# Two-part accumulation for the B, C and inner-channel streams, and a reworked decay, in a hybrid SSD trunk

## Chip, cores and metric

The kernel runs on one core of one Trainium2 chip. The metric is device time in microseconds of one execution; lower is better. Runs shown before are given as median, lowest and highest of three.

## What is computed

A trunk of two layers over 256 tokens and 2048 channels in float32. Layer 0 mixes tokens with a Mamba-2 state-space mixer (SSD), layer 1 with a short gated convolution; each is followed by a gated convolutional feed-forward block, and an RMSNorm closes. The change lies in the SSD mixer:

```python
def ssd_mixer(u, w_in, conv_w, conv_b, dt_bias, a_log, d_skip, norm_w, w_out):
    z, xbc, dt_raw = split(u @ w_in)                 # 4096 | 4096 + 1024 + 1024 | 64 columns
    xbc = silu(causal_dwconv(xbc, conv_w, conv_b))   # width 4
    xs, bm, cm = split(xbc)                          # inner channels, B, C (8 groups x 128 states)
    dt = softplus(dt_raw + dt_bias); a = -exp(a_log)
    y = ssd_chunked(xs, dt, a, bm, cm)               # two chunks of 128 tokens, 64 heads
    ...
# in ssd_chunked
    cs = cumsum(dt * a)                              # per head and chunk, falls
    decay[l, s] = exp(cs[l] - cs[s]) for s <= l, else 0
    y_diag = (C B^T * decay) @ (x * dt)
```

## The kernel before

**Precision by parts.** Every weight tile and every activation is split into a high part (a cast to the matmul's float32r format) and a low remainder. A product is then high x high + high x low + low x high: weight high against activation high and low, weight low against activation high. An activation tile `hl` holds its high part in columns 0 to 255 (the 256 tokens) and its low part in columns 256 to 511.

**Weights.** `plan` lists all 880 weight units in the order in which they are used; a unit is 256 rows by 512 columns (two blocks `k` of 128 rows, four blocks `t` of 128 columns). SyncE (SP) issues one 512 KB DMA per unit into `raw` (4 buffers). ScalarE casts it to `wh` (L302), VectorE subtracts for `wl` (L303); `wh` and `wl` have 4 buffers each.

**Streams.** `stream()` (L323) does one product of 512 output columns over all 2048 input rows: 8 units, 64 steps `(t, k)`. Its sums lie in two PSUM tiles ("main", three buffers of two banks in all), one for each pair of column blocks. With `one=True` a step is three matmuls of 256 columns into the same 256 columns of the tile: weight high x activation high (L354), weight high x activation low (L355), weight low x activation high (L340). With `one=False` it is one matmul of 512 columns, high and low side by side (L357), and the one of 256 (L340); the tile then holds two parts that must be added. When the last unit is through, `evac` is called for each of the two tiles: `scaled(pt, r, True)` multiplies the 256 columns by the row norm in one VectorE instruction (L412), while `scaled(pt, r)` first copies the upper part out with ScalarE (L404), adds on VectorE (L406), and then multiplies (L415). Then follow the width-4 convolution (L426 on ScalarE, L428 on VectorE) and SiLU.

Four kinds of stream run in the mixer: B and C (`bc_stream`, four streams, each for four groups), the inner channels (`xs_stream`, one for each of 8 groups), the gate (`z_stream`, 8, `one=False`), and the output projection (`residual_stream`, `one=False`). The first B stream is special: it is interleaved by hand with the preparation of `x` (`before=x_pair`) and its order is pinned. The later parts of the trunk use `late_stream`, whose steps are always 512 + 256 columns.

**Decays.** `ssd_decay` (L661) makes the masked decay for two heads: a DMA on SP's queue spreads the cumulative sums of two heads over all partitions (`cbc`, 256 KB, two buffers); six VectorE instructions of 128 columns subtract or add the token's own sum and clip at zero (L668, L670, L672); one ScalarE instruction exponentiates 768 columns (L674); one VectorE instruction multiplies by C B^T (L676). It is called 32 times. The tiles `m` that it fills have three buffers and are read by the matmuls L707 and L715.

**Order.** The Tile framework makes the order on each engine from its own simulated timeline; the first stream's instructions are pinned, and the late streams' matmuls are chained by `follow`. Elsewhere the framework may interleave the matmuls of one stream with those of the next and with the small products of the SSD core.

Of the kernel before, what the change touches and what calls it, by code (L numbers as in the profile page):

```python
# [8 lines left out]
F32 = mybir.dt.float32  # L9
F32R = mybir.dt.float32r  # L10
I32 = mybir.dt.int32
AF = mybir.ActivationFunctionType
ALU = mybir.AluOpType
# [3 lines left out]
P = 128  # L17
T = 256
D = 2048
NKD = D // P  # L20
DI = 4096
NG = 8
GC = DI // NG
NH = 64
HPG = NH // NG
DS = 128
CONVD = DI + 2 * NG * DS
W_SSD = 4
# [11 lines left out]
def trunk_kernel(ctx, tc, a, out):  # L40
    nc = tc.nc
    mm = nc.tensor.matmul
    act = nc.scalar.activation
    tt = nc.vector.tensor_tensor
    stt = nc.vector.scalar_tensor_tensor
    ts = nc.vector.tensor_scalar
# [29 lines left out]
    def uid(s):  # L76
        n_id[0] += 1
        return f"{s}_{n_id[0]}"

    def pair_tmp(tag="tp", pool=None):  # L80
        return (pool or tmp).tile([P, 2, T], F32, tag=tag, name=uid(tag))
# [7 lines left out]
    xspool = mixer.enter_context(tc.tile_pool(name="xspool", bufs=3))  # L89
# [128 lines left out]
    def rep2(t):  # L218
        return t.unsqueeze(1).to_broadcast([P, 2, T])
# [72 lines left out]
    def load_unit():  # L292
        i = len(units)
        if i == len(raws):
            load_raw()
        raw, raws[i] = raws[i], None
        wh = wpool.tile([P, KU, COLS], F32R, tag="wh", name=uid("wh"))
        wl = wpool.tile([P, KU, COLS], F32R, tag="wl", name=uid("wl"))
        units.append((wh, wl))

        def half(ks, put):
            put(nc.scalar.copy(wh[:, ks, :], raw[:, ks, :]))  # L302
            put(tt(  # L303
                out=wl[:, ks, :], in0=raw[:, ks, :], in1=wh[:, ks, :].bitcast(F32),
                op=ALU.subtract,
            ))

        if i == 0:
            return half
        with tc.high_priority(0 if i < NKD // KU else None):  # L310
            half(slice(0, KU), pin if i < NKD // KU + 2 else lambda ins: ins)

    def weight_unit(c0, kc, ahead=WB - 1):

        i = taken[0]
        assert plan[i][1:] == (c0, kc), (plan[i], c0, kc)
        taken[0] += 1
        while len(units) < min(i + ahead + 1, len(plan)):
            load_unit()
        got, units[i] = units[i], None  # L320
        return got

    def stream(c0, hls, kcs, evac, one=False, before=None):  # L323

        pts = [psm.tile([P, 2, 512], F32, tag="main", name=uid("main")) for _ in range(2)]
        n = len(kcs)
        put = (lambda ins: ins) if before is None else pin  # L330
        for u in range(0, n, KU):
            order = [(t, k) for t in range(4) for k in range(KU)]
            if before is not None and u == 0:
                before(0)
                order.sort(key=lambda tk: tk[1])
            wh, wl = weight_unit(c0, kcs[u], WB - 1 if before is None else 0)

            def low(t, k):
                i = u + k
                put(mm(  # L340
                    pts[t // 2][:, t % 2, 0:T], wl[:, k, t * P : (t + 1) * P],
                    hls[i // 2][:, i % 2, 0:T], start=False, stop=(i == n - 1),
                ))

            for at, (t, k) in enumerate(order):
                if before is not None and at == (0 if u else 2) and u + KU < n:
                    before(u // KU + 1)
                i = u + k
                o = pts[t // 2][:, t % 2, :]
                hl = hls[i // 2][:, i % 2, :]  # L350
                lw = slice(t * P, (t + 1) * P)
                first = i == 0
                if one:
                    put(mm(o[:, 0:T], wh[:, k, lw], hl[:, 0:T], start=first, stop=False))  # L354
                    put(mm(o[:, 0:T], wh[:, k, lw], hl[:, T : 2 * T], start=False, stop=False))  # L355
                else:
                    put(mm(o, wh[:, k, lw], hl, start=first, stop=False))  # L357
                if before is not None:
                    low(t, k)
                elif k == KU - 1:  # L360
                    for q in range(KU):
                        low(t, q)
        if before is not None:
            before(n // KU)
        if taken[0] < len(plan):
            while len(units) < min(taken[0] + WB - 1, len(plan)):
                load_unit()
        for p in range(2):
            evac(p, pts[p])
# [39 lines left out]
    def scaled(pt, r, one=False, tag="tp", pool=None):  # L409
        if one:  # L410
            s = pair_tmp(tag, pool)
            tt(out=s, in0=pt[:, :, 0:T], in1=rep2(r), op=ALU.mult)  # L412
            return s
        s = pair_sum(pt)
        tt(out=s, in0=s, in1=rep2(r), op=ALU.mult)  # L415
        return s

    def conv(s, width, wname, nk, k0, bname=None, tag="tp", pool=None):

        y = pair_tmp(tag, pool)  # L420
        for j in range(2):
            w = pcol(wname, (width - 1) * nk + k0 + j)
            if bname is None:
                act(y[:, j, :], s[:, j, :], AF.Copy, scale=w)
            else:
                act(y[:, j, :], s[:, j, :], AF.Identity, bias=pcol(bname, k0 + j), scale=w)  # L426
            for d in range(1, width):
                stt(  # L428
                    out=y[:, j, d:T], in0=s[:, j, 0 : T - d],
                    scalar=pcol(wname, (width - 1 - d) * nk + k0 + j),  # L430
                    in1=y[:, j, d:T], op0=ALU.mult, op1=ALU.add,
                )
        return y
# [27 lines left out]
    xp, xhl = [], []  # L461
    ss = small.tile([P, 2, 4], F32, tag="ss", name="ss")
    first = {}
# [48 lines left out]
    NCX = CONVD // P  # L512

    def bc_stream(g, o, before=None):

        res = []

        def evac(p, pt):
            k0 = DI // P + o * NG + g + 2 * p
            s = scaled(pt, first["r0"], True)  # L520
            y = conv(s, W_SSD, "ssdw", NCX, k0, "ssdb", "bc", bcpool)
            act(y, y, AF.Silu)
            res.append(y)

        stream(2 * DI + o * NG * DS + g * DS, xhl, range(NKD), evac, True, before)
        return res

    load_raw()
# [9 lines left out]
    for _ in range(2):  # L538
# [3 lines left out]
        out=dtw, in_=s_in[:, DI + CONVD :].rearrange("(k p) h -> p k h", p=P)  # L542
    ))

    def row_bcast(src, n, tag):
# [8 lines left out]
    r_tok, r0 = first["r_tok"], first["r0"]  # L554
# [4 lines left out]
        out=dtw, in0=dtw,  # L559
        in1=prm[i0][:, o0 : o0 + NKD].unsqueeze(2).to_broadcast([P, NKD, NH]), op=ALU.mult,  # L560
# [20 lines left out]
    for c in range(2):  # L581
        stt(
            out=v[:, c * NH : (c + 1) * NH], in0=ps[:, c * NH : (c + 1) * NH],
# [22 lines left out]
    cs = cpool.tile([P, 2, NH], F32, tag="cs", name="cs")  # L606
# [3 lines left out]
    rem = cpool.tile([P, NH], F32, tag="rem", name="rem")  # L610
# [14 lines left out]
    sp = mixer.enter_context(tc.tile_pool(name="sp", bufs=2))  # L625
    decpool = mixer.enter_context(tc.tile_pool(name="decpool", bufs=3))

    def xs_stream(g):
        res = [None, None]

        def evac(p, pt):
            y = conv(scaled(pt, r0, True), W_SSD, "ssdw", NCX, g * 4 + 2 * p, "ssdb", "xs", xspool)
            act(y, y, AF.Silu)
            res[p] = y

        stream(DI + g * GC, xhl, range(NKD), evac, True)
        return res

    def z_stream(g):
# [19 lines left out]
        return cb  # L659

    def ssd_decay(g, part, cb):  # L661
        h0 = g * HPG + part * 2
        cbc = sp.tile([P, 2, 2, P], F32, tag="cbc", name=uid("cbc"))
        nc.sync.dma_start(out=cbc, in_=cs_d[:, h0 : h0 + 2, :].partition_broadcast(P))
        m = decpool.tile([P, 2, 3, P], F32, tag="decay", name=uid("decay"))
        for h in range(2):
            hi = h0 + h
            ts(out=m[:, h, 0, :], in0=cbc[:, 0, h, :], scalar1=cs[:, 0, hi : hi + 1], scalar2=0.0,  # L668
               op0=ALU.subtract, op1=ALU.min)
            ts(out=m[:, h, 1, :], in0=cbc[:, 1, h, :], scalar1=rem[:, hi : hi + 1], scalar2=0.0,  # L670
               op0=ALU.add, op1=ALU.min)
            ts(out=m[:, h, 2, :], in0=cbc[:, 1, h, :], scalar1=cs[:, 1, hi : hi + 1], scalar2=0.0,  # L672
               op0=ALU.subtract, op1=ALU.min)
        act(m, m, AF.Exp)  # L674
        mf = m.rearrange("p h j l -> p h (j l)")
        tt(  # L676
            out=mf, in0=mf,
            in1=cb.rearrange("p j l -> p (j l)").unsqueeze(1).to_broadcast([P, 2, 3 * P]),
            op=ALU.mult,
        )  # L680
        return m
# [87 lines left out]
    for g in range(NG):  # L769
# [5 lines left out]
        m = [ssd_decay(g, part, cb) for part in range(4)]  # L775
        xs = xs_stream(g)
# [44 lines left out]
    xhl, nhl = nhl, []  # L821
# [11 lines left out]
    xhl, nhl = nhl, []  # L833
# [32 lines left out]
    xhl = nhl  # L866
# [30 lines left out]
    for part in range(2):  # L897
        lo, hi = FPARTS[part]
        hid = ffn_part(1, part, xhl, r)
        n = hi - lo  # L900
        for cg in range(D // COLS):
            cols = slice(cg * COLS, (cg + 1) * COLS)
            pt = psm.tile([P, 2, 512], F32, tag="main", name=uid("main"))
# [66 lines left out]
```

## Time and profile before

| | before |
|---|---|
| median of 3 runs | 2550.66 us (2550.61 to 2550.82) |
| profiled execution, its own time | 2550.66 us |
| profiled execution, span from first to last instruction | 2548.9 us |
| matrix engine (PE) busy | 2531.7 us, 99% |
| weight loads (PEld) busy | 2227.2 us, 87% |
| VectorE (DVE) busy | 1795.7 us, 70% |
| ScalarE (ACT) busy | 1317.4 us, 52% |
| mean granted clock of the matrix engine | 0.998 |

In the profile's rows PE is the matrix engine, PEld its weight loads, DVE is VectorE, ACT ScalarE, SPq the queue of SyncE. A row of a group names the line, engine, operation, output and inputs, shapes and count, then busy time and mean length of one, then the idle time before it and what ended that. Matmuls overlap, and the length of one is modelled; the distance between the starts of two is what counts for the pace. A row of a window gives, for each engine, the busy time and (in brackets) the number of instructions that touch the window.

The mixer takes about the first 708 us of the span; the streams that the change touches lie between 42 and 589 us.

### The profile page before, as it was taken

To read this page: it belongs to the slowest core of one execution; us is meant where nothing else is said; L and a number is where in the kernel's file an instruction comes from. 1 tells how busy PE (TensorE), PEld (TensorE's weight loads), DVE (VectorE), ACT (ScalarE), POOL (GpSimd) and SP (SyncE) were. 2 spreads that over 40 slices of the span, in tenths; PEclk is the share of its full clock that TensorE was granted. 3 is DMA by queue.
4 is the path that set the end of the run, shared out by engine and by line. 5 is a ranking of instruction groups with operands and counts; after the bars stand their busy time and mean duration, and the time that the engine had idled before them with its cause. 6 is when DMAs were issued, how large, how long until landed. Compare 5 with 4: busy or idle time off the path is not lost.

```text
span 2548.9 us, 38320 instructions
## 1 busy us (share of the span) xinstructions
PE 2531.7 (99%) x15101; PEld 2227.2 (87%) x15101; DVE 1795.7 (70%) x2601; ACT 1317.4 (52%) x1622; POOL 1.1 (0%) x8
## 2 busy tenths in 40 slices
PE   9999999999999999999999999999999999999998
PEld 9999998998888888888888888888888888888886
DVE  7798875888677776557776666666677764577764
ACT  5565543566555554345554444444555553455543
POOL 0000000000000000000000000000000000000000
PEclk9999999999999999999999999999999999999999
DMA  7566655665666666666666666666666666666664
GB/s 231 173 184 197 183 177 187 195 180 176 200 182 190 190 190 190 190 187 188 189 189 190 189 185 189 190 190 190 175 190 190 190 191 194 187 190 190 190 195 143
DMA packets 255736, 478.76 MB, mean 188 GB/s; under 512 B 17667, under 2 KB 29123, under 8 KB 255427
## 3 DMA queue, kind: packets, MB, share of 16 engines
q1 hardware_dynamic: 254643, 474.13, 62.7%
q8 instruction: 118, 1.93, 0.3%
q10 hardware_dynamic: 912, 2.18, 0.2%
q14 instruction: 63, 0.52, 0.1%
HBM read 474.09 MB, written 2.16 MB: 187 GB/s over the span
## 4 chain that ended last, share of the span: by engine, by line
PE 98%; DMA 1%; DVE 1%; ACT 0%; SPq 0%; issue 0%; DVEq 0%
PE main L385 41%; PE main L387 21%; PE main L357 9%; PE main L340 8%; PE main L354 4%; PE main L355 4%; PE main L915 3%; PE main L916 3%; PE main L917 3%; PE aux L707 1%; DMA raw<-in_ssd_w_in_dram 0%; DMA cbc<-cs_d 0%; PE aux L715 0%; PE aux L571 0%; PE aux L688 0%; PE aux L202 0%
## 5 line engine op out<-in xcount | busy, mean ns | idle before, releaser
L303 DVE TENSOR_TENSOR wl<-raw,wh 128x1024 fp32r<-128x1024 f32 (+1 forms) x881 | 1075.6, 1222 | 690.6 <-ACT wh L302 686.1
L302 ACT CAST wh<-raw 128x1024 fp32r<-128x1024 f32 (+1 forms) x881 | 923.4, 1049 | 1087.9 <-PE main L385 630.0
L385 PE MATMUL main<-hl,wh 128*128 128x512 f32 x4544 | 1427.5, 395 | 0.0
L387 PEld LDWEIGHTS main<-hl,wl 128*128 128x128 f32 x4544 | 853.4, 188 | 201.0
L387 PE MATMUL main<-hl,wl 128*128 128x256 f32 x4544 | 893.6, 278 | 0.0
L385 PEld LDWEIGHTS main<-hl,wh 128*128 128x128 f32 x4544 | 691.6, 189 | 0.1
L340 PE MATMUL main<-hl,wl 128*128 128x256 f32 x1792 | 362.0, 282 | 1.3 <-DVE wl L303 1.1
L340 PEld LDWEIGHTS main<-hl,wl 128*128 128x128 f32 x1792 | 311.0, 190 | 47.7 <-issue 3.3
L357 PE MATMUL main<-hl,wh 128*128 128x512 f32 x1024 | 321.4, 397 | 0.8 <-DVE hl L233 0.8
L354 PE MATMUL main<-hl,wh 128*128 128x256 f32 x768 | 204.3, 286 | 2.5 <-DVE tp L412 1.3
L355 PE MATMUL main<-hl,wh 128*128 128x256 f32 x768 | 203.3, 285 | 0.3
L357 PEld LDWEIGHTS main<-hl,wh 128*128 128x128 f32 x1024 | 157.5, 189 | 3.2 <-DVE hl L233 1.0
L354 PEld LDWEIGHTS main<-hl,wh 128*128 128x128 f32 x768 | 147.9, 193 | 3.5 <-issue 2.1
L355 PEld LDWEIGHTS main<-hl,wh 128*128 128x128 f32 x768 | 147.9, 193 | 1.1 <-DVE hl L233 0.7
L915 PE MATMUL main<-wh,hl 128*128 128x512 f32 x352 | 137.5, 391 | 0.8 <-DVE xtok L921 0.8
L916 PE MATMUL main<-wl,hl 128*128 128x512 f32 x352 | 137.5, 391 | 0.0
L917 PE MATMUL main<-wh,hl 128*128 128x512 f32 x352 | 136.9, 389 | 0.0
L404 ACT COPY tp<-main 128x512 f32<-128x512 f32 x128 | 74.3, 580 | 30.5 <-PE main L387 29.5
L406 DVE TENSOR_TENSOR tp<-main,tp 128x512 f32<-128x512 f32 x128 | 87.8, 686 | 1.3 <-ACT tp L404 1.2
L428 DVE SCALAR_TENSOR_TENSOR tp<-tp,prm,tp 128x255 f32<-128x255 f32 x208 | 88.5, 478 | 0.0
L915 PEld LDWEIGHTS main<-wh,hl 128*128 128x128 f32 x352 | 66.1, 188 | 15.4 <-DVE xtok L921 1.2
L917 PEld LDWEIGHTS main<-wh,hl 128*128 128x128 f32 x352 | 66.1, 188 | 14.1
(138 smaller groups left out, 1209.9 us busy)
## 6 DMA issues: line engine op xcount, KB each, us to landing
raw<-in_ffn_w_up_dram SPq DMA_DIRECT2D x352, 512.0 KB, 3.7
raw<-in_ffn_w_down_dram SPq DMA_DIRECT2D x176, 512.0 KB, 3.7
raw<-in_ssd_w_in_dram SPq DMA_DIRECT2D x159, 512.0 KB, 4.5
raw<-in_sc_w_in_dram SPq DMA_DIRECT2D x96, 512.0 KB, 4.0
raw<-in_ssd_w_out_dram SPq DMA_DIRECT2D x64, 512.0 KB, 4.1
raw<-in_sc_w_out_dram SPq DMA_DIRECT2D x32, 512.0 KB, 3.7
cbc<-cs_d SPq DMA_DIRECT2D x32, 256.0 KB, 5.6
xt<-in_x_dram SPq DMA_DIRECT2D x8, 256.0 KB, 7.1
```

Of the source, the lines that this page charges most:

```text
L302: put(nc.scalar.copy(wh[:, ks, :], raw[:, ks, :]))
L303: put(tt(out=wl[:, ks, :], in0=raw[:, ks, :], in1=wh[:, ks, :].bitcast(F32), op=ALU.subtract,))
L340: put(mm(pts[t // 2][:, t % 2, 0:T], wl[:, k, t * P : (t + 1) * P], hls[i // 2][:, i % 2, 0:T], start=False, stop=(i == n - 1),))
L354: put(mm(o[:, 0:T], wh[:, k, lw], hl[:, 0:T], start=first, stop=False))
L355: put(mm(o[:, 0:T], wh[:, k, lw], hl[:, T : 2 * T], start=False, stop=False))
L357: put(mm(o, wh[:, k, lw], hl, start=first, stop=False))
L385: follow(mm(o, wh[:, k, lw], hl, start=(i == 0), stop=False))
L387: follow(mm(o[:, 0:T], wl[:, k, lw], hl[:, 0:T], start=False, stop=(i == n - 1)))
L428: stt(out=y[:, j, d:T], in0=s[:, j, 0 : T - d], scalar=pcol(wname, (width - 1 - d) * nk + k0 + j), in1=y[:, j, d:T], op0=ALU.mult, op1=ALU ...
L915: follow(mm(pt[:, c, :], hi_, wh[:, k, :], start=(i == 0), stop=False))
L916: follow(mm(pt[:, c, :], hi_, wl[:, k, :], start=False, stop=False))
L917: follow(mm(pt[:, c, :], lo_, wh[:, k, :], start=False, stop=(i == n - 1)))
```

## The change

- In `bc_stream`, `one` becomes true only for the first B stream (the one with `before`). The other three B and C streams, and all 8 inner-channel streams, run with `one=False`, and their evacuation adds the two parts.
- In `ssd_decay` one VectorE subtraction over both heads and both chunks (512 columns, into a new tile `cbd`) replaces the four subtract-and-clip instructions; ScalarE clips it (Relu) and exponentiates it with scale -1 into the two diagonal parts; the part that joins the chunks is exponentiated straight from `cbc` with `rem` as the bias, one instruction for each head, without a clip.

```diff
@@ bc_stream
-            s = scaled(pt, first["r0"], True)
+            s = scaled(pt, first["r0"], before is not None)
...
-        stream(2 * DI + o * NG * DS + g * DS, xhl, range(NKD), evac, True, before)
+        stream(2 * DI + o * NG * DS + g * DS, xhl, range(NKD), evac, before is not None, before)
@@ xs_stream
-            y = conv(scaled(pt, r0, True), W_SSD, "ssdw", NCX, g * 4 + 2 * p, "ssdb", "xs", xspool)
+            y = conv(scaled(pt, r0), W_SSD, "ssdw", NCX, g * 4 + 2 * p, "ssdb", "xs", xspool)
...
-        stream(DI + g * GC, xhl, range(NKD), evac, True)
+        stream(DI + g * GC, xhl, range(NKD), evac)
@@ ssd_decay
         m = decpool.tile([P, 2, 3, P], F32, tag="decay", name=uid("decay"))
+        cbd = sp.tile([P, 2, 2, P], F32, tag="cbd", name=uid("cbd"))
+        tt(
+            out=cbd, in0=cs[:, :, h0 : h0 + 2].unsqueeze(3).to_broadcast([P, 2, 2, P]),
+            in1=cbc, op=ALU.subtract,
+        )
         for h in range(2):
-            hi = h0 + h
-            ts(out=m[:, h, 0, :], in0=cbc[:, 0, h, :], scalar1=cs[:, 0, hi : hi + 1], scalar2=0.0,
-               op0=ALU.subtract, op1=ALU.min)
-            ts(out=m[:, h, 1, :], in0=cbc[:, 1, h, :], scalar1=rem[:, hi : hi + 1], scalar2=0.0,
-               op0=ALU.add, op1=ALU.min)
-            ts(out=m[:, h, 2, :], in0=cbc[:, 1, h, :], scalar1=cs[:, 1, hi : hi + 1], scalar2=0.0,
-               op0=ALU.subtract, op1=ALU.min)
-        act(m, m, AF.Exp)
+            act(m[:, h, 1, :], cbc[:, 1, h, :], AF.Exp, bias=rem[:, h0 + h : h0 + h + 1])
+        act(cbd, cbd, AF.Relu)
+        act(m[:, :, 0:3:2, :], cbd.rearrange("p c h l -> p h c l"), AF.Exp, scale=-1.0)
```

## The prediction

> **What bounds the kernel.** I read the page's head first, then the matmul groups, then windows cut out of single streams, and last who waits for whom. The head:
>
> ```profile
> span 2548.9 us, 38320 instructions
> ...
> PE 2531.7 (99%) x15101; PEld 2227.2 (87%) x15101; DVE 1795.7 (70%) x2601; ACT 1317.4 (52%) x1622; POOL 1.1 (0%) x8
> ...
> PEclk9999999999999999999999999999999999999999
> ```
>
> The matrix engine is busy nearly all the time at the full granted clock. So time is won only where its own pace gets faster, and lost only where it is made to wait. The groups show which matmuls the change touches:
>
> ```profile
> L357 PE MATMUL main<-hl,wh 128*128 128x512 f32 x1024 | 321.4, 397 | 0.8 <-DVE hl L233 0.8
> L354 PE MATMUL main<-hl,wh 128*128 128x256 f32 x768 | 204.3, 286 | 2.5 <-DVE tp L412 1.3 <-ACT hl L232 1.2
> L355 PE MATMUL main<-hl,wh 128*128 128x256 f32 x768 | 203.3, 285 | 0.3
> ```
>
> L354 and L355 are the three-matmul steps (768 = 12 streams x 64); L357 is the step of 512 + 256. Mean lengths (286 + 285 against 397 ns) would promise 174 ns a step, but the matmuls overlap and their ends are modelled, so I don't use them. The pace is read from windows cut from start to start. The first row below is a whole group of the mixer, the second lies in an inner stream (L354, L355, twice, then two L340: 17 such rounds of two steps), the third in an output stream (two L357, two L340: 17 rounds as well), the fourth spans B and C streams:
>
> ```profile
> core 0: us, PE busy (x) PEld busy (x) DVE busy (x) ACT busy (x) POOL busy (x), PEclk, DMA share, GB/s
> 196.80:248.20 51.40, 51.40 (x375) 46.96 (x374) 45.60 (x94) 30.08 (x38) 0.00 (x0) 1.00 0.64 182
> 304.43:316.67 12.24, 12.24 (x105) 12.24 (x103) 9.86 (x24) 7.34 (x8) 0.00 (x0) 1.00 0.61 179
> 655.16:667.01 11.85, 11.85 (x71) 10.34 (x70) 7.57 (x9) 6.15 (x9) 0.00 (x0) 1.00 0.72 232
> 300.80:347.20 46.40, 46.40 (x388) 46.35 (x388) 38.13 (x67) 24.73 (x32) 0.00 (x0) 1.00 0.60 181
> ```
>
> The counts include up to three matmuls that cross an edge: 17 x 6 = 102 and 17 x 4 = 68 start inside. So 34 steps take 12.24 us in three matmuls and 11.85 us in two: 0.3600 against 0.3485 us a step, for the same 768 columns. The reason stands in the PEld column: with three matmuls the weight loads are busy for all of 12.24 us, and every matmul starts 12.24 / 102 = 0.120 us after the last one; with two they are busy for 10.34 of 11.85 us. The step pays for a third weight load, of the very weights just loaded.
>
> **Part 1: the streams' matmuls.** 11 of the 12 streams change (the first B stream keeps its three): 11 x 64 = 704 steps, each 0.3600 - 0.3485 = 0.0115 us shorter: 8.1 us. All of it is on the path, since PE is without gaps there (below). 704 matmuls go, so PE's count should fall from 15101 to 14397. Bounds of this term: 0, if the pace hung on the place and not on the number of loads, and 8.1 us.
>
> The Trainium skill, in "TensorE: Matmul & The Clock Gate", section "Back-to-back issue gap", gives about N/2.4 + 2.5 ns for an isolated matmul of N columns at full clock. Two of 256 would take 218.4 ns by it and one of 512 215.8, so that 704 steps would win an estimated 1.8 us and not 8.1. The trace disagrees, with 120 ns for each of 256.
>
> **Part 2: the evacuations.** 22 tiles (11 streams x 2) get a copy, an add and a multiply where there was one multiply. Rows for these and for the decays:
>
> ```profile
> L412 DVE TENSOR_TENSOR tp<-main,rrow 128x512 f32<-128x512 f32 x24 | 16.3, 684 | 1.9 <-PE main L340 1.1 <-ACT rrow L472 0.6
> L404 ACT COPY tp<-main 128x512 f32<-128x512 f32 x128 | 74.3, 580 | 30.5 <-PE main L387 29.5 <-PE main L340 0.8
> L406 DVE TENSOR_TENSOR tp<-main,tp 128x512 f32<-128x512 f32 x128 | 87.8, 686 | 1.3 <-ACT tp L404 1.2
> L415 DVE TENSOR_TENSOR tp<-tp,rrow 128x512 f32<-128x512 f32 x96 | 66.3, 690 | 2.4
> L668 DVE TENSOR_SCALAR decay<-cbc,cs 128x128 f32<-128x128 f32 x64 | 18.0, 281 | 11.0 <-DMA cbc<-cs_d 6.7 <-PE aux L715 3.9
> L670 DVE TENSOR_SCALAR decay<-cbc,rem 128x128 f32<-128x128 f32 x64 | 17.9, 280 | 0.0
> L672 DVE TENSOR_SCALAR decay<-cbc,cs 128x128 f32<-128x128 f32 x64 | 17.9, 279 | 0.0
> L674 ACT ACTIVATE decay<-decay 128x768 f32<-128x768 f32 x32 | 27.0, 844 | 7.0 <-DVE decay L672 6.9
> L676 DVE TENSOR_TENSOR decay<-decay,cb 128x768 f32<-128x768 f32 x32 | 29.1, 952 | 2.1 <-ACT decay L674 2.0
> L674 ACT ACT_TABLE_LOAD x11 | 14.1, 1283 | 16.0 <-DVE decay L672 16.0
> L646 ACT ACTIVATE z<-z 128x512 f32<-128x512 f32 x16 | 9.7, 627 | 4.6 <-DVE z L645 4.5
> L589 ACT ACTIVATE dt_e<-dt_e 128x128 f32<-128x128 f32 x1 | 0.3, 308 | 0.0
> L426 ACT ACTIVATE xs<-tp,prm,prm 128x256 f32<-128x256 f32 x32 | 16.8, 592 | 4.8 <-DVE tp L412 4.8
> L232 ACT ACTIVATE hl<-x,prm 128x256 fp32r<-128x256 f32 x64 | 28.7, 496 | 3.4 <-DVE x L486 1.9 <-DVE prm L165 1.3
> ```
>
> ScalarE gains 22 x 0.580 = 12.8 us, VectorE 22 x (0.686 + 0.690 - 0.684) = 15.2 us. On the path this costs something only if the next stream lacks its PSUM tile: three tiles exist, the ended stream holds two, and each is now held through a copy and an add, where it was one multiply. The gate streams already do just this, ahead of an inner stream:
>
> ```profile
> 219.57 0.59 ACT L404 COPY tp<-main 128x512 f32<-128x512 f32 x1
> ...
> 220.77 0.28 PE L354 MATMUL main<-hl,wh 128*128 128x256 f32 x1
> ...
> 221.73 0.58 ACT L404 COPY tp<-main 128x512 f32<-128x512 f32 x1
> ...
> 223.07 0.28 PE L354 MATMUL main<-hl,wh 128*128 128x256 f32 x1
> ...
> 223.26 0.68 DVE L406 TENSOR_TENSOR tp<-main,tp 128x512 f32<-128x512 f32 x1
> ...
> 226.19 0.68 DVE L406 TENSOR_TENSOR tp<-main,tp 128x512 f32<-128x512 f32 x1
> ```
>
> The inner stream starts at 220.77; the gate's tiles come free only at 223.94 and 226.87, over 3 us and 6 us later. PE shows no idle time there: the framework orders the first column pair's matmuls of several units ahead of the second pair's. PE's own waits from 93 to 670 us, all of them:
>
> ```profile
> PE main L357 <- DVE hl L233: 0.8, 1, 0.8
> PE aux L164 <- DVE prm L165: 0.3, 1, 0.3
> ```
>
> I take 0 for the release. Bounds: 0 and the price under rival C.
>
> **Part 3: the decays.** VectorE loses 18.0 + 17.9 + 17.9 = 53.8 us and gains 32 subtractions of 512 columns, 32 x 0.686 = 22.0 (L406's length; the broadcast form isn't in the trace, and I bound it by one L672, 0.279, and the six instructions that it replaces, 1.68): 31.8 us less. ScalarE loses 27.0 us. It gains, per call, two Exp of 128 columns (L589's 0.308, plus 0.096 for the bias operand, the difference of L426 with two operands and L232 with one: 0.404 each), a Relu and an Exp of 512 columns (0.627 each, L646): 2.06 us, 66.0 us in all, 39 us more. Relu has no row; between L404's 0.580 and L674's 0.844 it hardly matters. If every call's Relu cost one more table load, that would be 32 x 1.283 = 41 us more on ScalarE, off the path too as long as the lead of the weights holds (below).
>
> "ScalarE: Activation LUTs", section "Table sets: the hidden batching unit", in the Trainium skill says that cheap functions such as relu sit in every set; no row here can show it.
>
> Sum of parts 2 and 3: VectorE 16.6 us less, ScalarE 52 us more. In the fullest row, 196.80:248.20, with four calls and two tiles, VectorE goes from 45.60 to 45.60 - 4.0 + 1.4 = 43.0 us and ScalarE from 30.08 to 30.08 + 4.9 + 1.2 = 36.1 us, of about 50.7. Neither bounds. What hides them is the weights' lead:
>
> ```profile
> L303 DVE TENSOR_TENSOR wl<-raw,wh 128x1024 fp32r<-128x1024 f32 x879 | 1074.3, 1224 | 690.6 <-ACT wh L302 686.1 <-DMA prow<-in_ssd_conv_w_dram 0.5
> L302 ACT CAST wh<-raw 128x1024 fp32r<-128x1024 f32 x879 | 922.1, 1050 | 1085.9 <-PE main L385 630.0 <-PE main L917 126.3 <-PE main L357 115.2
> ...
> ACT wh L302 <- PE main L357: 85.4, 63, 5.2
> ACT wh L302 <- PE main L355: 53.5, 32, 2.3
> ...
> SPq L664 <- DVE decay L672: 33.3, 24, 3.4
> ```
>
> The casts wait for PE to give buffers back, so they are ahead of it: with four buffers and 2.8 us a unit (8 x 0.3485), a cast and its subtraction (1.05 + 1.22 us) have about 8 us. Work that comes in between for 2 us costs nothing. If that lead went, the 52 us of ScalarE would come onto the path up to their size.
>
> Queues: the decays' DMA stays, 32 issues on SP. Its buffer was released by L672; now by the later of the subtraction and the two Exp from `cbc`, which wait for a tile `m` just as L672 did. Behind it on SP are the weight loads, which wait for `raw` buffers anyway. From the last L715 that frees an `m` to the next L707, 6 x 0.28 + 0.844 + 0.952 becomes 4 short steps of which two no longer need `m`; nothing longer. 0 on the path.
>
> **Sum.** 2550.66 (the profiled execution's own time, equal to the median; 1.8 us of it outside the span) - 8.1 + 0 + 0 = 2542.6 us.
>
> **Rivals.**
> A, the forecast: 2542.6 us, with 2540 to 2545.5 for a scheduling that comes out otherwise by 2 or 3 us (PE's present waits in the mixer, about 1 us, could go too).
> B, columns alone set the pace: equal columns, equal time, 2550.7 us. For it: between L357s two L340 of 256 columns take 655.86 - 655.63 = 0.23 us, hardly less than the one of 512 (0.3485 - 0.115 = 0.2335):
>
> ```profile
> 655.63 0.39 PE L340 MATMUL main<-hl,wl 128*128 128x256 f32 x2
> 655.86 0.62 PE L357 MATMUL main<-hl,wh 128*128 128x512 f32 x2
> ```
>
> Against it: the windows 304.43 and 655.16, at the same clock. The rule on the issue gap is this case, give or take its 1.8 us.
> C, slower: the PSUM tile. A tile is held longer by the copy and by queueing, 3.1 us between the end of the copy at 220.16 and the add at 223.26. If PE waits for it at each of the 11 streams, the price is up to 11 x 3.1 = 34 us, giving 2576; it makes the kernel measurably slower from (8.1 + 5.1) / 11 = 1.2 us a stream on. For it: L354's row holds a wait of 1.3 us for L412, just such a tile. Against it: the gate streams, 8 of them, without one.
> D, the same mechanism or late casts, but small: 0.3 to 1.2 us a stream, 2546 to 2555.
>
> **How the numbers follow.** A 0.76, B 0.04, C 0.07, D 0.13, of which 0.03 still lies under 2545.5. A difference of 0.2%, 5.1 us, is about what a measurement of this kernel can tell from none. Faster is A and a little of D, 0.80 with rounding; same is B and the rest of D, 0.13; slower is C, 0.07. The range goes from 2540 up into D, to 2548.5.
>
> **What would show it.** PE near 14397 instructions; L357 x1728, L354 and L355 x64 each; windows in inner streams at 0.3485 us a step, with PEld no longer full; PE's waits in the mixer still about 1 us; everything after 700 us as before, but 8 us earlier. A wait of PE for L406 or for wl L303 after an inner stream would prove me wrong, as would steps at 0.360.

## The result, and the profile after

The changed kernel takes 2583.67 us (median of 4 runs, 2579.94 to 2586.18), the kernel before 2550.74 us in the same session (2550.61 to 2550.83). The ratio is 1.0128, with a 95% interval of 1.011 to 1.0145: 33 us slower, and 41 us above the forecast. The profiled execution took 2579.94 us, its span 2578.0 us. From the head of its page and the shares of its chain of waits:

```profile
span 2578.0 us, 36900 instructions
PE 2536.4 (98%) x14397; PEld 2195.1 (85%) x14397; DVE 1788.0 (69%) x2463; ACT 1354.8 (53%) x1738; POOL 1.1 (0%) x8
PE 93%; DMA 3%; DVE 1%; ACT 1%; issue 1%; SPq 0%; DVEq 0%; ACTq 0%
```

Before, that last row began with 98% for PE and 1% for DMA. PE's idle time (span less busy) went from 2548.9 - 2531.7 = 17.2 us to 2578.0 - 2536.4 = 41.6 us: 24.4 of the 29.1 us by which the span grew. The other 4.7 us lie inside the busy time, where a gain and a new loss meet. The gain is the one forecast. A window of an inner stream, cut from start to start (columns: length; busy time and count of PE, PEld, DVE, ACT, POOL; granted clock; DMA):

```profile
core 0: us, PE busy (x) PEld busy (x) DVE busy (x) ACT busy (x) POOL busy (x), PEclk, DMA share, GB/s
329.97:341.11 11.14, 11.14 (x66) 9.72 (x65) 9.25 (x19) 7.64 (x9) 0.00 (x0) 1.00 0.64 186
155.36:158.78 3.42, 3.42 (x12) 3.03 (x13) 3.39 (x5) 2.24 (x4) 0.00 (x0) 0.50 0.78 210
```

The first row holds 16 rounds of two steps: 11.14 / 32 = 0.348 us a step, with the weight loads no longer full. Over 704 steps that is about the forecast 8.1 us. The second row is the new loss: 3.42 us at a granted clock of 0.50. Busy time grew by 4.7 us though the pace gained 8.1, so about 12.8 us more were spent on the same columns, most of it in such stretches (some 9 to 10 us, an estimate from the distances between the matmuls' starts from 45 to 720 us).

Who waits for whom, in the first 720 us, all engines and then PE:

```profile
DVE cbd L668 <- DMA cbc<-cs_d: 54.6, 25, 4.1
ACT cbd L674 <- DVE cbd L668: 23.8, 14, 3.0
ACT decay L673 <- DMA cbc<-cs_d: 22.5, 9, 4.6
PE aux L209 <- DVE nacc L739: 16.7, 6, 3.9
PE aux L689 <- DVE cb L658: 2.6, 1, 2.6
PE main L340 <- DVE wl L303: 2.0, 2, 1.1
```

The kernel before had one row of the first kind, and an eighth as long:

```profile
DVE decay L668 <- DMA cbc<-cs_d: 6.7, 6, 3.4
```

VectorE, whose busy time fell, now stands still for 54.6 us waiting for the transfer of the cumulative sums. One such wait and what it does, from the timeline of the changed kernel (start, length, engine; in brackets the idle time before it and its releaser; rows between are left out):

```profile
150.50 0.68 DVE L733 TENSOR_TENSOR yg<-yg,z 128x512 f32<-128x512 f32 x1
...
151.22 0.63 ACT L735 ACTIVATE tp<-yg 128x512 f32<-128x512 f32 x1 [0.43 <-DVE yg L733]
...
152.33 0.69 DVE L668 TENSOR_TENSOR cbd<-cs,cbc 128x512 f32<-128x512 f32 x1 [1.14 <-DMA cbc<-cs_d]
152.94 1.22 DVE L303 TENSOR_TENSOR wl<-raw,wh 128x1024 fp32r<-128x1024 f32 x1
153.05 0.63 ACT L674 ACTIVATE cbd<-cbd 128x512 f32<-128x512 f32 x1 [1.20 <-DVE cbd L668]
153.59 1.03 ACT L302 CAST wh<-raw 128x1024 fp32r<-128x1024 f32 x1
154.07 0.68 DVE L737 TENSOR_TENSOR tp<-tp,tp 128x512 f32<-128x512 f32 x1
...
154.79 0.42 DVE L739 TENSOR_TENSOR nacc<-tp 128x256 f32<-128x256 f32 x1
...
155.36 0.77 PE L209 MATMUL aux<-ones,nacc 128*128 128x1 f32 x3 [3.52 <-DVE nacc L739]
```

Read it from the bottom. PE idles 3.52 us for L739, the gate's sum of squares. L739 needs the sum L737, which needs the square that ScalarE made from 151.22 on and had ready at 151.85. VectorE stood idle then and could have gone on. But at the head of its queue stood the decay's subtraction L668, which does not need any of this and waited for its DMA until 152.33; behind it in the queue stood a weight subtraction (L303), and L737 came 2.2 us late, about half of it by the rest of the wait and by L668 itself and half by L303. ScalarE stood behind the same instruction for 1.20 us: its clip L674 was next in its own queue, and a cast (L302) behind that. The second row of windows above is what follows: PE starts again at half clock.

The order on VectorE is alike in the other groups. PE waits for L739 in six groups, and in five of them a subtraction L668 stands between L733 and L739; in the sixth (before 612.17) it stands ahead of L733 and of what feeds it, and waited 2.60 us there. It is there because the subtractions run further ahead: when the gate's sum of the first seven groups goes, the changed kernel has done the subtractions of 9, 13, 17, 21, 25, 29 and 32 calls, the kernel before those of 7, 11, 15, 19, 23, 27 and 31.

The half clock of that second row recurs. Apart from one at the very start (7.3 us), the halved stretches in the mixer begin at 123.36, 154.08, 263.30, 321.33 and 666.08 us and last 3.41 or 6.83 us; all but the last lie on, or right behind, an idle time of PE of 2.62, 3.52, 3.89 and 2.98 us, the last behind two of 1.45 and 1.84 us close together. Two idle times of 2.91 us (before 209.92) and 2.58 us (before 612.17) were not followed by one. "TensorE: Matmul & The Clock Gate" in the Trainium skill, section "Why this matters for your kernels", warns of idle gaps over about 3 us between bursts, after which the clock falls to half. The traces agree for the long ones, since all of 2.98 us and more, in all runs here, were followed by a halved stretch; below that they differ: single idle times of 1.45 us (e5_clip_on_dve, before 547.62), 1.57 us (e6_decays_in_place, before 200.17) and 1.84 us (e11_last_stream_one, before 633.23) were followed by one too. The last section shows what goes with them. A halved stretch of 3.41 us in which PE has work costs 1.7 us on top of the idle time.

### The profile page after: what moved, and what is told of

Its sections match the earlier page's. It is cut to its first block, busy times and chain, and to the rows that moved or that the text cites. A ratio compares the mean times of both kernels' runs of the same rounds, so it can differ in the third digit from the quotient of the medians.

```text
span 2578.0 us, 36900 instructions
## 1 busy us (share of the span) xinstructions
PE 2536.4 (98%) x14397; PEld 2195.1 (85%) x14397; DVE 1788.0 (69%) x2463; ACT 1354.8 (53%) x1738; POOL 1.1 (0%) x8
## 3 DMA queue, kind: packets, MB, share of 16 engines
q8 instruction: 112, 1.84, 0.3%
## 4 chain that ended last, share of the span: by engine, by line
PE 93%; DMA 3%; DVE 1%; ACT 1%; issue 1%; SPq 0%; DVEq 0%; ACTq 0%
PE main L385 41%; PE main L387 20%; PE main L357 13%; PE main L340 7%; DMA cbc<-cs_d 3%; PE main L916 3%; PE main L917 3%; PE main L918 3%; PE aux L708 0%; DVE wl L303 0%; PE aux L689 0%; PE aux L571 0%; DMA raw<-in_ssd_w_in_dram 0%; ACT decay L673 0%; PE aux L209 0%
## 5 line engine op out<-in xcount | busy, mean ns | idle before, releaser
L303 DVE TENSOR_TENSOR wl<-raw,wh 128x1024 fp32r<-128x1024 f32 (+1 forms) x881 | 1076.2, 1223 | 682.6 <-ACT wh L302 678.4
L302 ACT CAST wh<-raw 128x1024 fp32r<-128x1024 f32 (+1 forms) x881 | 922.7, 1048 | 1026.7 <-PE main L385 627.9
L385 PE MATMUL main<-hl,wh 128*128 128x512 f32 x4544 | 1427.5, 395 | 0.0
L387 PEld LDWEIGHTS main<-hl,wl 128*128 128x128 f32 x4544 | 853.5, 188 | 201.0
L385 PEld LDWEIGHTS main<-hl,wh 128*128 128x128 f32 x4544 | 691.6, 189 | 0.1
L357 PE MATMUL main<-hl,wh 128*128 128x512 f32 x1728 | 550.8, 401 | 3.1 <-DVE hl L233 1.8
L340 PEld LDWEIGHTS main<-hl,wl 128*128 128x128 f32 x1792 | 336.3, 191 | 77.3 <-DVE wl L303 3.2
L357 PEld LDWEIGHTS main<-hl,wh 128*128 128x128 f32 x1728 | 270.5, 191 | 10.6 <-issue 5.8
L406 DVE TENSOR_TENSOR tp<-main,tp 128x512 f32<-128x512 f32 x150 | 102.9, 686 | 1.6 <-ACT tp L404 1.6
L404 ACT COPY tp<-main 128x512 f32<-128x512 f32 x150 | 86.9, 580 | 32.1 <-PE main L387 29.5
L415 DVE TENSOR_TENSOR tp<-tp,rrow 128x512 f32<-128x512 f32 x118 | 81.5, 690 | 2.5
L917 PEld LDWEIGHTS main<-wl,hl 128*128 128x128 f32 x352 | 66.1, 188 | 13.5
L428 DVE SCALAR_TENSOR_TENSOR g<-tp,prm,g 128x254 f32<-128x254 f32 (+1 forms) x176 | 73.1, 477 | 0.0
L668 DVE TENSOR_TENSOR cbd<-cs,cbc 128x512 f32<-128x512 f32 x32 | 22.1, 691 | 55.4 <-DMA cbc<-cs_d 54.6
```

Of the source, the lines that this page charges most:

```text
L303: put(tt(out=wl[:, ks, :], in0=raw[:, ks, :], in1=wh[:, ks, :].bitcast(F32), op=ALU.subtract,))
L340: put(mm(pts[t // 2][:, t % 2, 0:T], wl[:, k, t * P : (t + 1) * P], hls[i // 2][:, i % 2, 0:T], start=False, stop=(i == n - 1),))
L385: follow(mm(o, wh[:, k, lw], hl, start=(i == 0), stop=False))
L387: follow(mm(o[:, 0:T], wl[:, k, lw], hl[:, 0:T], start=False, stop=(i == n - 1)))
L404: nc.scalar.copy(pb, pt[:, :, T : 2 * T])
L406: tt(out=s, in0=pt[:, :, 0:T], in1=pb, op=ALU.add)
```

## The experiments

The letters in the expectations: T, the subtraction blocks VectorE's queue while it waits for its DMA; S, the cause is ScalarE; P, the PSUM tile (the prediction's rival C); N, the small operations of the gate's norm on VectorE. Diffs are against the changed kernel unless said.

**The two halves alone.** e1_streams has the new streams and the old decays, e2_decays the old streams and the new decays.

> The streams' half of the change alone; the decays as before. Theory T (VectorE's queue is blocked at its head by the new subtraction, which waits for the DMA of cbc): nothing of the loss is here, 2542.6 us (2541 to 2545), steps at 0.3485 us, PE idle in the mixer about 1 us. Rival P (the PSUM tiles are held longer by copy and add, and PE waits for them): the loss is here, 2575 to 2585 us. Rival S (ScalarE's longer chain in the decays delays the casts): 2542.6 us as well.

> The decays' half alone; the streams keep three matmuls of 256. T: the whole loss and no gain, 2551 + 41 = 2592 us (2580 to 2595), VectorE waiting some 50 us for cbc. Rival P: 2551 us, no loss. Rival S: 2592 us as T.

e1_streams: 2559.99 us, ratio 1.0036 (1.0023 to 1.0049). e2_decays: 2591.87 us, ratio 1.0166 (1.0149 to 1.0183). The decays are most of the loss, as T says; but the streams lose too, where the forecast had them gain 8 us, and neither expectation had that number. The two losses overlap: 9.0 and 40.9 us alone, 32.9 together. The waits of e2_decays:

```profile
DVE cbd L668 <- DMA cbc<-cs_d: 49.3, 20, 4.2
PE aux L209 <- DVE nacc L739: 15.9, 6, 3.1
```

They are those of the full change. PE's longest of e1_streams from 93 us on are others:

```profile
PE main L357 <- DVE tp L406: 4.8, 2, 3.9
PE aux L202 <- DVE dg L194: 2.8, 1, 2.8
PE aux L209 <- DVE nacc L738: 2.5, 1, 2.5
```

The first is the prediction's rival C, a wait for the PSUM tile, but once at length (3.9 us, before 305.87) and not in each of 11 streams. The others stand at the mixer's end, where PE has nothing else to do. Why the end comes late is seen on VectorE. In the kernel before, the norm of gate 6 (rsqrt from its first approximation L180 to the last step L188, eleven tiny instructions that depend on each other) runs nearly in one piece:

```profile
585.46 0.17 DVE L180 TENSOR_SCALAR rs_i<-var 128x2 int32<-128x2 int32 x1
...
587.40 1.23 DVE L303 TENSOR_TENSOR wl<-raw,wh 128x1024 fp32r<-128x1024 f32 x1 [0.40 <-ACT wh L302]
...
590.04 0.15 DVE L188 SCALAR_TENSOR_TENSOR rs_r<-rs_t,rs_r 128x2 f32<-128x2 f32 x1
```

In e1_streams its first few instructions take turns with convolutions and weight subtractions that stand between them in VectorE's queue:

```profile
596.14 0.16 DVE L180 TENSOR_SCALAR rs_i<-var 128x2 int32<-128x2 int32 x1
596.22 0.87 DVE L428 SCALAR_TENSOR_TENSOR xs<-tp,prm,xs 128x254 f32<-128x254 f32 x2
597.00 1.22 DVE L303 TENSOR_TENSOR wl<-raw,wh 128x1024 fp32r<-128x1024 f32 x1
...
606.13 0.16 DVE L188 SCALAR_TENSOR_TENSOR rs_r<-rs_t,rs_r 128x2 f32<-128x2 f32 x1
```

That is 10.1 us instead of 4.7. The norm also begins 10.7 us later than before (596.14 against 585.46), and why it does was not settled; so its own length is 5.4 of the 15.2 us by which what follows is late. The last product of the SSD core (L707, L715) starts at 635.8 us instead of 620.6, and the following window shows a PE that is idle for a third of the time and at 0.79 of its clock (before: 23.23 us busy of the same 24, at 1.00):

```profile
628.00:652.00 24.00, 16.36 (x89) 12.73 (x88) 14.10 (x37) 7.61 (x11) 0.00 (x0) 0.79 0.34 123
```

**Put the wait for `m` back.** In the kernel before, the first decay instruction wrote into `m`, so that it could go only when a matmul had given an `m` back. The new subtraction writes `cbd` and is free of that. e3_in_place lets it work in `m`:

```diff
-        tt(out=cbd, in0=cs[...]..., in1=cbc, op=ALU.subtract)
+        tt(out=m[:, :, 0:3:2, :].rearrange("p h c l -> p c h l"), in0=cs[...]..., in1=cbc, op=ALU.subtract)
...
-        act(cbd, cbd, AF.Relu)
-        act(m[:, :, 0:3:2, :], cbd.rearrange("p c h l -> p h c l"), AF.Exp, scale=-1.0)
+        act(m[:, :, 0:3:2, :], m[:, :, 0:3:2, :], AF.Relu)
+        act(m[:, :, 0:3:2, :], m[:, :, 0:3:2, :], AF.Exp, scale=-1.0)
```

> Both halves, but the subtraction writes straight into the decay tile m, and Relu and Exp work in place there; cbd is gone. The same instructions, yet the subtraction must wait for m again, as the six instructions before did, so that it is queued on VectorE later than its DMA lands. T: the waits of VectorE for cbc fall from 54.6 to under 10 us, PE's waits for the gate's sums vanish, 2543 us (2541 to 2549). Rival P: 2584 us, no change. Rival S: ScalarE does the same work in the same order, 2575 to 2585 us.

2554.91 us, ratio 1.0016 (1.0006 to 1.0025). The same instructions on the same engines, another tile, and with it another order: 29 of the 33 us are gone.

```profile
DVE decay L667 <- DMA cbc<-cs_d: 16.1, 7, 3.3
PE aux L202 <- DVE dg L194: 2.8, 1, 2.8
PE aux L209 <- DVE nacc L738: 1.9, 2, 1.7
```

VectorE's wait for the DMA falls from 54.6 to 16.1 us, PE's for the gate's sum from 16.7 to 1.9 us. The order is the old one again too: 7, 11, 15, 19, 23, 27 and 31 calls when the gate's sums go. It is still 12 us above the 2543 expected and outside the expected range, and the 16.1 us miss the 10 expected. e6_decays_in_place does the same to e2_decays:

> The decays' half alone, streams of three matmuls as before, and the subtraction written in place into m, as in e3. Theory T (the decays lose only by the subtraction's early place in VectorE's queue): 41 us of loss in e2 fall to nearly nothing, 2551 us (2549 to 2556). Rival S (ScalarE's longer chain): still over 2570 us. If it stays between, both have a share.

2564.3 us, ratio 1.005 (1.0035 to 1.0066). Of the 41 us that e2_decays lost, 27.6 are gone, 13 stay; the expected range was missed. Its wait for the DMA is 19.8 us, 8 times, and the longest of PE's waits is one that e2_decays has too (4.9 us; the kernel before 0.3). Below it a row of VectorE's timeline just ahead of it:

```profile
PE aux L164 <- DVE prm L165: 4.3, 1, 4.3
113.79 1.23 DVE L303 TENSOR_TENSOR wl<-raw,wh 128x1024 fp32r<-128x1024 f32 x1 [3.24 <-ACT wh L302]
```

It lies in the first group. The copy L165 stands on VectorE behind that L303, and the cast that L303 waits for starts only at 112.73 on ScalarE, behind table loads and the decays' Exp and Relu. So both have a share, as the expectation says for a time in between: here it is ScalarE's longer chain that is late. The 4.3 us and the halved stretch of 6.83 us on and behind them make some 7 to 8 of the 13 us, an estimate.

**Take ScalarE out.** e5_clip_on_dve leaves `cbd` and lets VectorE clip, right behind the subtraction:

```diff
-        act(cbd, cbd, AF.Relu)
+        ts(out=cbd, in0=cbd, scalar1=0.0, scalar2=None, op0=ALU.max)
```

> Both halves, but the clip of cbd is done by VectorE and not by ScalarE (Relu gone). T: the subtraction still stands ahead of the gate's work with its wait for cbc, 2575 to 2590 us. Rival S: ScalarE is relieved of 20 us and of a hop, so at least half of the loss goes, under 2563 us. Rival P: 2584 us.

2568.53 us, ratio 1.0066 (1.0051 to 1.0081): between the two expectations. VectorE waits for the DMA as often as in the full change, but the gate's sum is hardly late:

```profile
DVE cbd L668 <- DMA cbc<-cs_d: 46.4, 27, 3.9
ACT decay L675 <- DVE cbd L674: 5.6, 7, 2.3
PE main L340 <- DVE wl L303: 7.5, 7, 1.5
PE aux L209 <- DVE nacc L739: 3.3, 2, 1.8
```

So the blocked queue hurts along two paths. The subtractions run as far ahead as in the full change (9, 13, 17 and so on), and VectorE waits nearly as long. ScalarE's own wait for it is down from 23.8 to 5.6 us and half of the 33 us went with that; the other half stays with VectorE's wait, and part of it falls on the weights' remainders (`wl`, 7.5 us). The split is read from the waits; the framework's order changes with the edit, and the two were not separated.

**The DMA earlier.** If what is left in e3_in_place is the wait for the transfer, then two more `cbc` buffers, which let SP issue it earlier, should take it away (e12_cbc_four, against e3_in_place: `cbc` with `bufs=4`).

> e3 (both halves, subtraction in place) with four buffers for cbc in place of two, so that the four transfers of a group can all be issued a group ahead. Theory T (what is left of the decays' loss in e3 is VectorE and ScalarE waiting for cbc, 16 and 20 us): both waits fall under 8 us and the time by some 2 to 5 us, 2551 us (2549 to 2554). If the rest is the late last gate alone: 2554 to 2556 us as e3, whatever the waits do.

2552.59 us, ratio 1.0005 (0.9996 to 1.0014).

```profile
DVE decay L667 <- DMA cbc<-cs_d: 5.4, 2, 4.2
ACT decay L672 <- DMA cbc<-cs_d: 5.6, 2, 3.5
```

VectorE's wait falls from 16.1 to 5.4 us, ScalarE's from 19.8 to 5.6, and the time by 2.3 us, as T expected. The medians are 2.3 us apart and the intervals of the two ratios meet (1.0006 to 1.0025 against 0.9996 to 1.0014), so the direction is likely and its size is not settled. The rest of e3's loss is not this wait.

**What a stall does to the clock.** e7_stall_ladder is the kernel before with 22 stalls of graded length in the late streams: a tiny matmul, a chain of tiny VectorE instructions on its result, and a matmul on that.

> The kernel before, with 22 waits put between the streams of the feed-forward blocks: a matmul, a chain of 0, 4, 8 ... 28 tiny VectorE instructions, and a matmul that needs the last. PE is idle for some 0.5 to 6 us each time. If idle time itself halves the granted clock (theory C), the clock's record shows halved stretches only behind the longer waits, from about 2 to 3 us on, each costing 1.7 us or a multiple; the time is that of before plus the idle time plus half of the halved stretches. If the halved stretches seen so far have another cause, none or one shows here.

One run, 2798.94 us. The steps came out coarser than meant, 0.74 us and then 5.5 us and more, so the stretch of 1 to 5 us is left to the other runs. A window behind the shortest and one around the next:

```profile
747.00:760.00 13.00, 12.26 (x73) 10.71 (x72) 9.63 (x15) 6.46 (x9) 0.00 (x0) 1.00 0.59 186
1030.00:1050.00 20.00, 14.52 (x77) 12.67 (x76) 13.64 (x26) 9.52 (x13) 0.00 (x0) 0.83 0.36 108
```

After 0.74 us the clock stays at 1.00; after 5.48 us and each longer one (8.0, 9.3, 10.7 to 13.1 us) stretches of half clock of 6.83 to 13.65 us lie on the idle time and behind it. They begin 2.0 to 5.2 us after PE stops.

**The norm off VectorE.** To see whether the small operations are what e1_streams loses by, e8_streams_norm_on_gpsimd moves the three refinement steps of the gate's rsqrt to GpSimd, as four instructions each (against e1_streams):

```diff
+        if eng is nc.gpsimd:
+            for _ in range(3):
+                eng.tensor_tensor(out=t, in0=r, in1=r, op=ALU.mult)
+                eng.tensor_tensor(out=t, in0=t, in1=v, op=ALU.mult)
+                eng.tensor_scalar(out=t, in0=t, scalar1=-0.5, scalar2=1.5, op0=ALU.mult, op1=ALU.add)
+                eng.tensor_tensor(out=r, in0=t, in1=r, op=ALU.mult)
+            return r
...
-        r = mean_rsqrt(tok_sum(one), GC)
+        r = mean_rsqrt(tok_sum(one), GC, nc.gpsimd)
```

> The streams' half alone (e1), but the Newton steps of the gate's norm run on GpSimd and not between the convolution's instructions on VectorE. Theory N (in e1 the last gate comes late because its norm is spread between the longer evacuations on VectorE, and PE idles at the mixer's end): the 7.2 us of idle time at the end and the halved clock behind it vanish or shrink to 2 us, 2545 us (2542 to 2551). If the end of the mixer is late for another reason: 2557 to 2562 us, as e1.

> Both halves with the subtraction in place (e3), and the Newton steps of the gate's norm on GpSimd. Theory N: 2546 us (2543 to 2551), under the kernel before. Otherwise 2553 to 2557 us, as e3.

e8: 2549.5 us, ratio 0.9993 (0.9984 to 1.0002), 10.5 us less than e1_streams and inside N's range, though 4.1 us of idle time stay at the mixer's end where 2 were expected. All waits of PE from 93 us on:

```profile
PE aux L209 <- DVE dg L201: 2.3, 1, 2.3
PE main L364 <- DVE hl L240: 1.8, 1, 1.8
```

The wait for the PSUM tile is gone too, although nothing of the evacuation was changed. e9 (e3_in_place with the same edit): 2556.36 us, ratio 1.002 (1.0011 to 1.0029), no better than e3. N missed there: with the decays on ScalarE, something else holds. PE's longest idle times in e9 are those at the mixer's end, as in e8 (2.29 and 1.84 us, with a halved stretch of 6.83 us); it also idles in the first group, around 114 to 121 us, at 148 and at 186 us. Which wait sets the time was not settled.

The two waits left in e8 lie at the end of the mixer, where the last norm's latency is bare: its steps take 4.2 us on GpSimd (627.61 to 631.84). e10_norm_split keeps the last group's norm on VectorE; e11_last_stream_one also gives the last inner stream its three matmuls and short evacuation back (against e8):

```diff
+        r = mean_rsqrt(tok_sum(one), GC, nc.vector if g == NG - 1 else nc.gpsimd)   # e10, e11
...
+        stream(DI + g * GC, xhl, range(NKD), evac, g >= NG - 1)                     # e11, and scaled() alike
```

> The streams' half, the gate's Newton steps on GpSimd for the first seven groups (as e8), but on VectorE for the last one, where VectorE has nothing else to do and a step is shorter (0.2 us a step against 0.35 us). Theory N: the idle time of 2.3 us before the last norm's broadcast shrinks to about 1 us or less, 2548 us (2546 to 2550), just under the kernel before. Otherwise as e8, 2549.5 us.

> e10, and the last inner stream back to three matmuls with the short evacuation. Theory N: its chain into the last gate is shorter by a copy and an add, 64 steps cost 0.7 us more; the idle time at the mixer's end, 4 us in e8, shrinks by about 2 us: 2547 us (2545 to 2550). If the long evacuation has no part in the late end: 2549 us or more.

e10: 2547.12 us, ratio 0.9984 (0.9975 to 0.9992). e11: 2546.75 us, ratio 0.9982 (0.9973 to 0.9991). In e10 the first of the two waits has become

```profile
PE aux L209 <- DVE dg L201: 0.8, 1, 0.8
```

Both are about 4 us below the kernel before, their intervals just under 1, and neither beats the other. They are the streams' half with the old decays and the gate's norm moved: 8.1 us by the forecast, and half of it kept. In e10's profile PE is busy for 2524.0 us, 7.7 less than before (up to 1.7 of that is a halved stretch at the start that only the kernel before has), but idle for 2.4 us more.

## Why the prediction was wrong

**Part 1 held.** The pace in the streams is 0.348 us a step, PE's count is 14397, and L357 x1728 and L354 and L355 x64 each are in the groups. Rival B is out. That the third weight load is the reason for the slower pace stays the prediction's reading; no run separates it.

**The durations held; the loads of the engines were overstated.** The groups of the changed kernel:

```profile
L668 DVE TENSOR_TENSOR cbd<-cs,cbc 128x512 f32<-128x512 f32 x32 | 22.1, 691 | 55.4 <-DMA cbc<-cs_d 54.6 <-ACT decay L675 0.7
L673 ACT ACTIVATE decay<-cbc,rem 128x128 f32<-128x128 f32 x64 | 22.0, 391 | 26.7 <-DMA cbc<-cs_d 22.5 <-PE aux L716 4.0
L674 ACT ACTIVATE cbd<-cbd 128x512 f32<-128x512 f32 x32 | 19.9, 627 | 23.9 <-DVE cbd L668 23.8
L675 ACT ACTIVATE decay<-cbd 128x512 f32<-128x512 f32 x32 | 19.7, 619 | 0.2
```

The subtraction takes 691 ns (forecast 686), Exp with a bias 391 (404), Relu 627 and Exp 619 (627). Relu brought no table loads: L674 has no row of them, and the decays' own fell from 11 to 9 at L673 and 1 at L675. That is what "ScalarE: Activation LUTs" in the Trainium skill, section "Table sets: the hidden batching unit", says of cheap functions. Busy time moved by -7.7 us on VectorE and +37.4 us on ScalarE, against -16.6 and +52. The forecast added up lengths, but instructions that follow each other overlap a little: the six old ones occupied VectorE for 41.2 us in the kernel before, not 53.8. Neither engine became a bound by its sum.

**The step that failed: "0 on the path" in part 3, under the queues.** The prediction weighed how long each decay instruction is and what it waits for, and said that two of the new ones "no longer need `m`; nothing longer". That was named as harmless. It was the price. Without the wait for `m` the subtraction was placed early on VectorE, ahead of work that was ready, and it waited there for its DMA: 54.6 us. Where the prediction speaks of the release of `cbc`, it can even be read to put the subtraction among those that "wait for a tile `m` just as L672 did"; in the code the subtraction writes `cbd`. The order on VectorE (two calls further ahead) and e3_in_place show it: with the subtraction in `m` the old order and 29 us come back, with no other work changed. Half of the price went through ScalarE, which stood behind the same subtraction (e5_clip_on_dve).

**The cover was mis-sized.** The lead of the weights, some 8 us of slack, was taken as what hides VectorE and ScalarE. It does hide them from the streams' matmuls: PE waits 2.0 us for `wl` in all. It does not hide the small products of the gate, which stand in PE's own queue ahead of the streams (L209, 16.7 us). Here a stall on a side chain stopped the main one, since both share PE's queue. On top of six of PE's idle times came the clock, which the sum had no term for.

**"I take 0 for the release" in part 2 failed too**, by less. In e1_streams it should have given 2542.6 us and gave 2560.0. Rival C's wait exists (4.8 us in two places), but it is not what the loss is made of in the main: by the timelines the gate's norm comes late beside the longer evacuations, and the end of the mixer is left without cover. e8 and e10 take most of it away by moving the norm alone. That "the gate streams, 8 of them," go without a wait was evidence about a PSUM tile, not about eleven more evacuations on VectorE beside the gate's norm.

**The chances.** Slower had 0.07, all for rival C. The prediction's own bound, 52 us of ScalarE if the lead goes, held the result, but by luck: the lead did not go (2.0 us of waiting for `wl`). No rival asked what happens if an instruction that is now free of a wait meets another one at the head of its queue.

**Open.** What keeps e3_in_place, e9 and e12_cbc_four 5 to 10 us above e10, with ScalarE's heavier decays common to them, is not settled. The traces show where: from its first matmul up to 130 us PE idles 7.1, 5.5 and 8.4 us in them against 4.6 in e10, from 600 to 720 us 5.0, 4.1 and 5.0 against 2.7, with a halved stretch of 6.83 us at that end in each and none in e10. e10's split of the norm was not tried with the new decays. That GpSimd's norm helps e8 by taking latency off VectorE, and not by the different order that the framework then makes, is argued from the waits; the two were not separated.

## What to carry to other kernels

When an edit frees an instruction from a wait, ask what it waits for next and what is queued behind it: in an engine's queue as VectorE's was here, a ready instruction that stands behind one waiting for a DMA is late, however idle the engine looks. Size cover separately for each chain that meets in the bound engine's queue; the weights' lead covered the streams and not the gate's sums. And count a gap of about 1.5 us or more in the matrix engine as possibly more than itself: every gap from 2.98 us on brought a stretch at half clock here, and some of the shorter ones did.

## What the runs showed of the hardware

A halved stretch comes in units of 3.41 us (3.41, 6.83, 10.24, 13.65 us in these runs, the one behind the last matmul apart). The length of the idle time does not decide alone: 2.91 us went without one (the changed kernel, before 209.92), 2.62 us did not. All the stretches of a run begin on one grid of 3.413 us: in the changed kernel 34, 43, 75, 92 and 193 units behind the first. What went with them is how busy PE was in the unit before, by the modelled ends of its matmuls. Three units of the changed kernel, the first two around the 2.91 us, the third ahead of a halved stretch:

```profile
205.28:208.69 3.41, 1.72 (x10) 1.23 (x9) 3.38 (x6) 2.19 (x3) 0.00 (x0) 1.00 0.51 183
208.69:212.11 3.42, 2.19 (x14) 2.00 (x15) 3.20 (x5) 2.58 (x5) 0.00 (x0) 1.00 0.55 161
317.92:321.33 3.41, 0.43 (x4) 0.21 (x2) 2.11 (x5) 1.20 (x3) 0.00 (x0) 1.00 0.62 181
```

An idle time that an edge of the grid cuts in two leaves both units half busy. Over all profiles here, from 40 us to the last matmul, each of the 39 full-clock units in which PE was busy for 0.42 or less was followed by a half-clock one, none with 0.58 or more was, and 4 of the 16 between were.

"TensorE: Matmul & The Clock Gate" in the Trainium skill, section "Part 1: The HAM clock gate (the "warmup" mystery)", tells of a free-running window of 4096 cycles and of half rate after an idle one; 4096 cycles at its 1.2 GHz are an estimated 3.41 us, which is the unit seen, and the grid is what a window that runs by itself would give. The page speaks of an idle window; in these traces units in which PE worked for up to 0.57 of the time were followed by half clock too.

GpSimd takes some 0.2 us for most of the tiny operations of the norm, but some are slow: in e8, 61 of the 96 took under 0.25 us and 10 over 1 us, up to 1.45. VectorE's own mean for such operations in e8 is 159 to 162 ns. Shortest, median and longest in ns, then the first and the last start:

```profile
L188 POOL TENSOR_TENSOR rs_t<-rs_t,var x24: 195/198/1453, 150.7 to 631.1; 128x2 f32<-128x2 f32 x24
L189 POOL TENSOR_SCALAR rs_t<-rs_t x24: 191/193/1132, 151.1 to 631.4; 128x2 f32<-128x2 f32 x24
```

Moving them there paid all the same (e8 against e1_streams), for the reason left open above. At the end, where PE had none, VectorE looks better: 0.8 instead of 2.3 us of waiting in e10, and a median 2.4 us lower, though the intervals of e8 and e10 overlap.
